# Token values of the first mix, three held rows, norms tile after tile, and background steps at the middle and end of each weight tile

## The chip, the cores and the metric

One core of a Trainium2 chip runs the whole kernel. Its engines are TensorE (PE), VectorE (DVE), ScalarE (ACT), GpSimd (POOL) and the queue of SyncE (SP), which issues DMAs. The metric is the device time of one execution in microseconds: 2220.9 us, the median of three runs of the kernel before (2220.26 to 2222.0).

## The reference, cut to what matters

Two transformer blocks run over 256 tokens of width 1024, in float32. Each is a mixing layer with a residual, followed by a product-key expert layer (PEER) with a residual.

```python
h = rmsnorm(x, norm_mix_g)                       # block 1, first mix
rq, rk, rv, rg, dq, dk, dv = split(h @ w_in)     # 4 retention heads, 4 attention heads
ret = silu(rg) * rmsnorm(retention(rq, rk, rv))
att = rmsnorm(softmax(q1 k1) @ dv - lam * softmax(q2 k2) @ dv, g) * 0.8
x = x + concat(ret, att) @ w_out
x = x + peer(rmsnorm(x, norm_ffn_g), wq, subkeys, u, v)
x = rmsnorm(x, final_norm_g)
h = rmsnorm(x, norm1_2)                          # block 2: a gated delta rule and a gated
x = x + mix(h) @ w_out_2                         # linear recurrence, 80 column tiles of w_in_2
x = x + peer(rmsnorm(x, norm2_2), w_pq, sub_keys, u_2, v_2)
return rmsnorm(x, final_norm_2)
```

`peer` picks 16 experts per token and head from 128 x 128 keys. The kernel computes it densely: `gelu(x @ u.T)` for all 16384 experts, times a matrix of gates that is zero for all experts that were not picked, times `v`.

## The kernel before

Every weight matrix is a row of tiles of 128 x 1024 floats (512 KB). `plan` lists all of them in the order of use: 28 of the first mix's `w_in`, 8 of `w_out`, 16 of `wq`, 128 of `u`, 128 of `v`, then the same for block 2. SP loads a tile into a ring of three `raw` buffers (L151). ACT copies it rounded into `hi` (L159), DVE and POOL write the rest `lo = raw - hi` (L164, DVE the first 640 columns in the mixes, POOL the others), each in a ring of three buffers. `x` is split in the same way into `xh` and `xl`, and each product is the sum of three matmuls, `hi*xh`, `hi*xl` and `lo*xh`.

`tile_ch` (L197) multiplies one tile: its 8 chunks of 128 x 128 are the stationary operands, the 256 tokens stream past, 24 matmuls of 256 columns add up in one PSUM bank, and the result has channels on the partitions. `acc_tile` (L278) does it the other way round for `v` and the output projections: the activations are stationary, 512 columns of the weight stream, tokens are on the partitions, and two token tiles (tt) with two halves of 512 columns (dh) fill four banks.

The work between the big products is written as generators in `k.bg`. `pass_round` advances each of the first four or ten by one step, and a step usually holds one stage on one engine (a group of small matmuls, then the ACT or DVE operation that reads them). In the first mix and in `Mix2` two rounds stand behind each tile. The order of instructions on an engine is then made by a scheduler from the order in the program and its own estimates of times; `issue_after(i)` makes it keep what is in the block behind instruction i on that engine.

The first mix takes its 28 tiles in the order 4 x `rg`, then `dq dk dv` of each attention head, then `rq rk rv` of each retention head. `dv` is transposed to tokens by two matmuls against the identity per head (L702). `norm_first` normalises both token tiles: a diagonal matrix of the reciprocal roots times `x` (L349), then ACT and DVE copy the 8 chunks of both token tiles out (L353, L354). Three later norms (`norm` after each mix, `norm_twice` after the first expert layer) do for each token tile: add the projection to x (L289, L291), sum of squares on ACT (L296), times the gain (L370, L385, L389), reciprocal root on POOL (L308), diagonal matrix on DVE (L300), 8 matmuls that transpose (L323), `xh` on ACT (L325), `xl` on DVE (L326). A 128 x 128 product of plain float32 counts as two matmuls in the trace. `final` does the same without the transposes, and writes out.

An output projection or `v` holds its last rows back (`LAST = 2` of 128): all rows but those are added for both token tiles, then the held rows for token tile 0, then for token tile 1, so that token tile 0's sums are complete while PE still works on tile 1. The held weights stay in the `hi` and `lo` rings.

## Time and profile before

| what | value |
|---|---|
| median of three runs | 2220.9 us |
| the profiled execution | 2218.6 us, span 2216.8 us |
| PE busy | 2167.8 us, 98% of the span, 15512 matmuls |
| DVE, ACT, POOL busy | 69%, 52%, 37% |
| mean granted TensorE clock | 0.996 of full speed |
| DMA | 167 GB/s mean |

A busy share is of the whole span and hides single stages. The idle time of PE is the difference between a stretch and PE's busy time in it. A row of the timeline gives the start, the length, the engine, the line, the operation, its output and inputs, how many are merged, and in brackets how long the engine was idle before it and what ended that. Matmuls overlap: the row's length is that of one matmul from end to end, the distance between starts is what it costs.

### The profile page before, as it was taken

How to read it: one execution, taken by the hardware profiler on the slowest of the kernel's cores; microseconds unless marked ns; L12 is line 12 of the kernel's file. 1: busy time of each engine (PE TensorE's matmuls, PEld its weight loads, DVE VectorE, ACT ScalarE, POOL GpSimd, SP SyncE). 2: the span in 40 equal slices, each digit the busy share in tenths (PEclk: the TensorE clock that was granted, in tenths of full speed). 3: DMA queues.
4: the chain of work that ended last, by engine and by line, in shares of the span. 5: the costliest groups of instructions: out<-in, count | busy, mean ns of one | idle time of the engine just before them, and what ended most of it. 6: DMA issues, size and time to landing. Idle time of an engine off the chain costs nothing. (4 is left out here: it accounts for less than half of the span.)

```text
span 2216.8 us, 41395 instructions
## 1 busy us (share of the span) xinstructions
PE 2167.8 (98%) x15512; PEld 2016.0 (91%) x15512; DVE 1533.0 (69%) x3122; ACT 1154.8 (52%) x2183; POOL 813.5 (37%) x623
## 2 busy tenths in 40 slices
PE   8999999999999999989999999999999999999998
PEld 8989999999988888879899998999999999888887
DVE  5669986898644544477687787799778885444444
ACT  5645545444455555556455655455454445555554
POOL 3454000000065666646275675620000002665664
PEclk9999999999999999999999999999999999999999
DMA  5555655555556656534444244555555555665654
GB/s 188 155 176 162 185 170 167 157 162 161 172 190 207 200 192 196 193 118 137 131 123 135 68 143 152 173 162 185 178 162 158 157 160 183 193 206 190 195 194 152
DMA packets 103880, 370.89 MB, mean 167 GB/s; under 512 B 12928, under 2 KB 14080, under 8 KB 103424
## 3 DMA queue, kind: packets, MB, share of 16 engines
q1 hardware_dynamic: 101808, 365.21, 52.1%
q10 hardware_dynamic: 1872, 3.04, 0.5%
q8 instruction: 122, 2.00, 0.4%
q14 instruction: 78, 0.64, 0.1%
HBM read 367.16 MB, written 1.05 MB: 166 GB/s over the span
## 5 line engine op out<-in xcount | busy, mean ns | idle before, releaser
L164 POOL TENSOR_TENSOR lo<-raw,hi 128x384 fp32r<-128x384 f32 (+1 forms) x428 | 689.5, 1612 | 1309.1 <-ACT hi L159 1271.4
L159 ACT ACTIVATE hi<-raw 128x1024 fp32r<-128x1024 f32 x684 | 724.0, 1060 | 680.2 <-PE mm L197 403.4
L164 DVE TENSOR_TENSOR lo<-raw,hi 128x640 fp32r<-128x640 f32 (+1 forms) x654 | 668.0, 1022 | 313.5 <-ACT hi L159 306.2
L197 PE MATMUL mm<-xh,hi 128*128 128x256 f32 x2848 | 820.9, 288 | 4.4 <-DVE sg L866 2.9
L197 PE MATMUL mm<-xh,lo 128*128 128x256 f32 x2848 | 807.5, 284 | 0.3 <-DVE lo L164 0.2
L197 PE MATMUL mm<-xl,hi 128*128 128x256 f32 x2848 | 803.9, 282 | 0.9 <-DVE xl L326 0.7
L197 PEld LDWEIGHTS mm<-xh,hi 128*128 128x128 f32 x2848 | 538.2, 189 | 5.9 <-DVE sg L866 3.3
L197 PEld LDWEIGHTS mm<-xl,hi 128*128 128x128 f32 x2848 | 538.9, 189 | 1.8 <-DVE xl L326 1.1
L197 PEld LDWEIGHTS mm<-xh,lo 128*128 128x128 f32 x2848 | 534.8, 188 | 0.7 <-DVE lo L164 0.7
L278 PE MATMUL y<-lo,ah 128*128 128x512 f32 x1024 | 398.2, 389 | 0.0
L278 PE MATMUL y<-hi,ah 128*128 128x512 f32 x1024 | 397.4, 389 | 0.0
L278 PE MATMUL y<-hi,al 128*128 128x512 f32 x1024 | 275.9, 389 | 0.0
L635 DVE TENSOR_TENSOR al<-a,ah 128x256 fp32r<-128x256 f32 x256 | 118.1, 462 | 193.2 <-PE y L278 192.9
L278 PEld LDWEIGHTS y<-hi,al 128*128 128x128 f32 x1024 | 192.2, 188 | 39.9
L278 PEld LDWEIGHTS y<-lo,ah 128*128 128x128 f32 x1024 | 192.3, 188 | 39.8
L278 PEld LDWEIGHTS y<-hi,ah 128*128 128x128 f32 x1024 | 192.2, 188 | 39.8
L634 ACT ACTIVATE ah<-a 128x256 fp32r<-128x256 f32 x256 | 106.5, 417 | 168.3 <-PE y L278 166.7
L197 PE MATMUL wm<-xh,hi 128*128 128x256 f32 x320 | 92.1, 289 | 5.4 <-ACT sq L1059 2.1
L197 PE MATMUL wm<-xh,lo 128*128 128x256 f32 x320 | 90.6, 285 | 0.6 <-DVE lo L164 0.6
L197 PE MATMUL wm<-xl,hi 128*128 128x256 f32 x320 | 90.5, 283 | 0.3 <-DVE xl L326 0.3
L535 DVE TENSOR_TENSOR ow<-ow,w 128x1024 f16<-128x1024 f16 x128 | 87.1, 683 | 0.1
L563 ACT ACTIVATE a<-mm 128x256 f32<-128x256 f32 (+33 forms) x228 | 69.0, 302 | 0.0
(513 smaller groups left out, 2271.6 us busy)
## 6 DMA issues: line engine op xcount, KB each, us to landing
raw<-in_u_dram SPq DMA_DIRECT2D x256, 512.0 KB, 3.5
raw<-in_v_dram SPq DMA_DIRECT2D x256, 512.0 KB, 4.2
raw<-in_w_in_dram SPq DMA_DIRECT2D x108, 512.0 KB, 3.5
raw<-in_wq_dram SPq DMA_DIRECT2D x32, 512.0 KB, 3.7
raw<-in_w_out_dram SPq DMA_DIRECT2D x16, 512.0 KB, 3.6
raw<-in_w_branch_a_dram SPq DMA_DIRECT2D x8, 512.0 KB, 3.5
raw<-in_w_branch_b_dram SPq DMA_DIRECT2D x8, 512.0 KB, 3.6
skT<-in_sk_dram ACTq DMA_DIRECT2D x2, 1024.0 KB, 5.1
```

Source lines behind the costliest of these rows:

```text
L159: self.nc.scalar.activation(out=h, in_=r, func=ACTF.Copy)
L164: eng.tensor_tensor(out=l[:, a:b], in0=r[:, a:b], in1=h[:, a:b].bitcast(F32), op=ALU.subtract)
L197: self.nc.tensor.matmul(out=ps, lhsT=a[:, c, :], rhs=b, start=(c == 0 and k == 0), stop=(c == NC - 1 and k == 2))
L278: i = self.nc.tensor.matmul(out=self.y[tt][dh], lhsT=p[:, ts], rhs=q[:, ds], start=(first and m == 0), stop=(last and m == 2))
L535: nc.vector.tensor_tensor(out=ow[q], in0=ow[0], in1=some(self.w[:, q]), op=ALU.mult)
L563: nc.scalar.activation(out=a[:, s, n:T], in_=ps[:, n:T], func=ACTF.Gelu)
L634: nc.scalar.activation(out=h, in_=a, func=ACTF.Copy)
L635: nc.vector.tensor_tensor(out=l, in0=a, in1=h.bitcast(F32), op=ALU.subtract)
```

## The change

Five things are changed.

1. The four tiles of `dv` come first in the first mix, in another layout (`_quads`): each holds two chunks of 128 input channels times all 512 columns of `dv`. `tile_tok` makes x the stationary operand, so the result has tokens on its partitions and 512 columns, and needs no transposes (`vt`, one ACT copy per token tile). `norm_first` is called for one token tile at a time, and its ACT and DVE copies are per chunk and token tile (128 x 128).
2. The constants `sub`, `pr` and `lam` of the attention heads are computed three rounds later, behind the last gate product on DVE and the last sigmoid on ACT.
3. `LAST = 3`, and the held rows have buffers of their own (`hold`), in the space of `a1` once that is used up. The gains are loaded there at row 72 of 128 instead of row 40.
4. `turn`: in `norm`, `norm_twice` and `final` the add, the square and the gain of a half stand together, the second half behind the first, and token tile 1 behind token tile 0's diagonal matrix (or its scaling, in `final`).
5. In the first mix's heads and in `Mix2`, one `pass_round` is called in the middle of a tile's 24 matmuls and one at its end, instead of two at the end.

```diff
     def _conv(self):
...
-        h = self.ring.tile([P, D], FR, tag="hi", name="hi", bufs=HI)
+        if n in self.place:
+            h, l = self.place.pop(n)
+        else:
+            h, l = (self.ring.tile([P, D], FR, tag=t, name=t, bufs=b) for t, b in (("hi", HI), ("lo", LO)))
...
-    def tile_ch(self, xh=None, xl=None, tag=None):
+    def tile_ch(self, xh=None, xl=None, tag=None, mid=None):
...
+            if mid is not None and c == NC // 2 - 1:
+                mid()
...
+    def tile_tok(self, tt, w, n, y):
+        h, l = w
+        ts = slice(tt * P, (tt + 1) * P)
+        todo = [(x, b, c2) for x, bs in ((self.xh, (h, l)), (self.xl, (h,))) for c2 in range(2) for b in bs]
+        for m, (x, b, c2) in enumerate(todo):
+            self.last_mm = self.nc.tensor.matmul(out=y, lhsT=x[:, 2 * n + c2, ts], rhs=b[:, c2 * 512:c2 * 512 + 512],
+                                                 start=(n == 0 and m == 0), stop=(n == 3 and m == len(todo) - 1)).ins
+
+    def first_quads(self, norms):
+
+        self.prefetch(3)
+        norms[0]()
+        ws = [self.weights() for _ in range(3)]
+        self.quads = [self.bank([P, 512])]
+        for n in range(3):
+            if n == 2:
+                norms[1]()
+            self.tile_tok(0, ws[n], n, self.quads[0][1])
+        self.quads.append(self.bank([P, 512]))
+        for n in range(3):
+            self.tile_tok(1, ws[n], n, self.quads[1][1])
+            with self.tc.issue_after(self.last_act):
+                self.prefetch(n + 1)
+        w = self.weights()
+        for tt in range(2):
+            self.tile_tok(tt, w, 3, self.quads[tt][1])
...
+    def turn(self, tt, n):
+
+        return self.tc.issue_after(self.first_half) if n else self.tc.issue_after(self.behind) if tt else nullcontext()
...
-    def norm_first(self, g, xn):
+    def norm_first(self, tt, g, xn):
...
+        for c4 in range(2):
+            tag, ps = self.bank([P, 4, P])
+            with self.tc.issue_after(self.last_mm) if tt else nullcontext():
+                for c in range(4):
+                    cc = c4 * 4 + c
+                    nc.tensor.matmul(out=ps[:, c, :], lhsT=x[:, cc * P:(cc + 1) * P], rhs=dr, start=True, stop=True)
+            for c in range(4):
+                cc = c4 * 4 + c
+                h, gc = self.xh[:, cc, ts], g[:, cc:cc + 1]
+                last = nc.scalar.activation(out=h, in_=ps[:, c, :], func=ACTF.Copy, scale=gc)
...
     def norm(self, tt, gn, xg, xn):
...
         for dh in range(2):
             hs = self.half(dh)
-            self.add_half(tt, dh, None)
-            self.square(x[:, hs], xn[:, hs], s[dh])
-        for dh in range(2):
-            hs = self.half(dh)
-            nc.vector.tensor_tensor(out=xg[:, hs], in0=x[:, hs], in1=gn[:, hs], op=ALU.mult)
+            with self.turn(tt, dh):
+                self.add_half(tt, dh, None)
+                self.square(x[:, hs], xn[:, hs], s[dh])
+                self.first_half = nc.vector.tensor_tensor(out=xg[:, hs], in0=x[:, hs], in1=gn[:, hs], op=ALU.mult).ins
...
-LAST = 2
+LAST = 3
...
-                if n == 40:
-                    gs = [k.spread(row(m), g) for m, g in enumerate(self.gs)]
-                if n == 60 and len(gs) > 1:
+                if n == P - SPLIT + 8:
+
+                    ap1.__exit__(None, None, None)
+                    end = pool("end")
+                    row = lambda name, dt=F32: end.tile([P, D], dt, name=name)
+                    gs = [k.spread(row(f"g{m}"), g) for m, g in enumerate(self.gs)]
+                    scratch = [[row(f"x{tt}{m}") for m in range(1 + len(gs))] for tt in range(2)]
+                    k.hold(P - LAST - n, [(row(f"wh{m}", FR), row(f"wl{m}", FR)) for m in range(LAST)])
+                if n == P - 40 and len(gs) > 1:
...
-                k.prefetch()
-
-            held = [(k.weights(), a) for a in last]
+                k.prefetch(2 + (n > P - LAST - 5))
+
+            held = [(k.weights(), a) for a in parts]
...
-        k.norm_first(k.g, [pool.tile([P, D], F32, name="xn", tag="xn", bufs=2) for tt in range(2)])
-        k.prefetch_behind()
+        k.first_quads([lambda tt=tt: k.norm_first(tt, k.g, pool.tile([P, D], F32, name="xn", tag="xn", bufs=2)) for tt in range(2)])
+        vt = pool.tile([P, 2, 4, P], F32, name="vt")
+        for tt, (tag, ps) in enumerate(k.quads):
+            nc.scalar.activation(out=vt[:, tt].rearrange("p h n -> p (h n)"), in_=ps, func=ACTF.Copy)
+            k.done(tag)
+        k.prefetch()
...
-        nc.vector.tensor_scalar(out=sub, in0=sub, scalar1=1.0 - (0.8 - 0.6), scalar2=None, op0=ALU.mult)
...
-        def lam_last():
+        def lambdas():
             yield
             yield
+            yield
+            pr = pool.tile([P, 2, 64], F32, name="pr")
+            d2 = dl.rearrange("p (a two) b -> p a two b", two=2)
+            with k.tc.issue_after(gate):
+                nc.vector.tensor_tensor(out=pr, in0=d2[:, :, 0, :], in1=d2[:, :, 1, :], op=ALU.mult)
+                nc.vector.tensor_reduce(out=lam[:, 0:2], in_=pr, axis=AX.X, op=ALU.add)
+                nc.vector.tensor_scalar(out=sub, in0=sub, scalar1=1.0 - (0.8 - 0.6), scalar2=None, op0=ALU.mult)
+            with k.tc.issue_after(sig):
...
-                for n in "qkv":
-                    ps = k.tile_ch()
+                names = "qk" if kind == "d" else "qkv"
+                for n in names:
+                    ps = k.tile_ch(mid=lambda: pass_round(k, 4))
                     got.append(halves(ps) if kind + n == "dq" else taken(ps, kind + n))
-                    if n == "v":
+                    if n == names[-1]:
                         k.spawn(work(h, *got))
-                    pass_round(k, 4)
                     pass_round(k, 4)
...
+
+        mid = self.mid = lambda: pass_round(k, 10)
+
+        def after():
+            pass_round(k, 10)
...
-                ps, done = k.tile_wide()
+                ps, done = k.tile_wide(mid)
...
-            after(2)
+            after()
...
+def _quads(w):
+
+    return np.ascontiguousarray(w.reshape(4, 2, P, 512).transpose(0, 2, 1, 3)).reshape(4, P, D)
```

How the rows of an engine move is seen best at three places. First, PE at the start of the program: `by_93` to `by_96`, `by_112`, `by_125`, `by_158` and `bg_171` are banks of transposes, `by_138` is the bank of token tile 0's `dv`. Before:

```order
L349 MATMUL by_95<-xn,x 128x128 x2
L349 MATMUL by_96<-xn,x 128x128 x2
L197 MATMUL mm<-xh,hi 128x256
L197 MATMUL mm<-xl,hi 128x256
L197 MATMUL mm<-xh,lo 128x256
```

and now, from the first matmul of the program:

```order
L395 MATMUL by_112<-xn,x 128x128 x4
L395 MATMUL by_125<-xn,x 128x128 x4
L218 MATMUL by_138<-hi,xh 128x512
L218 MATMUL by_138<-lo,xh 128x512
L218 MATMUL by_138<-hi,xh 128x512
L218 MATMUL by_138<-lo,xh 128x512
L218 MATMUL by_138<-hi,xl 128x512 x2
L218 MATMUL by_138<-hi,xh 128x512
L218 MATMUL by_138<-lo,xh 128x512
L218 MATMUL by_138<-hi,xh 128x512
L218 MATMUL by_138<-lo,xh 128x512
L218 MATMUL by_138<-hi,xl 128x512 x2
```

Products stood behind the transposes of both token tiles; now 12 products of token tile 0 stand before the transposes of token tile 1.

Second, DVE at the norm after the second mix, from the halves of token tile 0 on. Before:

```order
L370 TENSOR_TENSOR xg<-x,gn 128x512 x2
L289 TENSOR_TENSOR x<-y,x 128x512
L371 TENSOR_SCALAR nrm<-nrm 128x1
L289 TENSOR_TENSOR x<-y,x 128x512
L370 TENSOR_TENSOR xg<-x,gn 128x512
L300 TENSOR_SCALAR xn<-k_ident,nrm 128x128
L370 TENSOR_TENSOR xg<-x,gn 128x512
L371 TENSOR_SCALAR nrm<-nrm 128x1
L300 TENSOR_SCALAR xn<-k_ident,nrm 128x128
L326 TENSOR_TENSOR xl<-bg_16445,xh 128x4x128
```

and now, from the second half of token tile 0 on:

```order
L328 TENSOR_TENSOR x<-y,x 128x512
L416 TENSOR_TENSOR xg<-x,gn 128x512
L417 TENSOR_SCALAR nrm<-nrm 128x1
L343 TENSOR_SCALAR xn<-k_ident,nrm 128x128
L328 TENSOR_TENSOR x<-y,x 128x512
L416 TENSOR_TENSOR xg<-x,gn 128x512
L328 TENSOR_TENSOR x<-y,x 128x512
L369 TENSOR_TENSOR xl<-bg_16398,xh 128x4x128
L416 TENSOR_TENSOR xg<-x,gn 128x512
L417 TENSOR_SCALAR nrm<-nrm 128x1
L369 TENSOR_TENSOR xl<-bg_16405,xh 128x4x128
L343 TENSOR_SCALAR xn<-k_ident,nrm 128x128
```

Both adds of token tile 1 stood ahead of token tile 0's diagonal matrix (`xn`); now they stand behind it, with two `xl` of token tile 0 between them and token tile 1's diagonal matrix.

Third, PE at the end of the program. `y_22760` and `y_22761` are token tile 0's two halves before, `y_22713` and `y_22714` now. Before:

```order
L278 MATMUL y_22760<-hi_25656,ah_25579 128x512
L278 MATMUL y_22761<-hi_25656,ah_25579 128x512
L278 MATMUL y_22760<-lo_25658,ah_25579 128x512
L278 MATMUL y_22760<-hi_25656,al_25580 128x512
L278 MATMUL y_22761<-lo_25658,ah_25579 128x512
L278 MATMUL y_22761<-hi_25656,al_25580 128x512
L278 MATMUL y_22762<-hi_25639,ah_25575 128x512
```

and now:

```order
L317 MATMUL y_22713<-wh2_24387,al_25593 128x512
L317 MATMUL y_22714<-wh0_24383,al_25585 128x512
L317 MATMUL y_22714<-wh1_24385,ah_25588 128x512
L317 MATMUL y_22714<-wl1_24386,ah_25588 128x512
L317 MATMUL y_22714<-wh1_24385,al_25589 128x512
L317 MATMUL y_22714<-wh2_24387,ah_25592 128x512
L317 MATMUL y_22714<-wl2_24388,ah_25592 128x512
L317 MATMUL y_22714<-wh2_24387,al_25593 128x512
L317 MATMUL y_22715<-wh0_24383,ah_25584 128x512
```

Token tile 0's halves were complete with 14 and 12 matmuls left to do; now they are with 25 and 18 left.

## Rows read from the trace of the kernel before

**Rows 1.** Stretches (us): length, busy (count) of PE, PEld, DVE, ACT, POOL; granted clock; DMA.

```profile
13.10:33.20 20.10, 16.97 (x124) 16.30 (x123) 11.05 (x22) 12.12 (x19) 9.08 (x6) 0.92 0.59 177
33.20:140.80 107.60, 107.27 (x789) 101.31 (x788) 66.83 (x110) 60.28 (x146) 46.56 (x38) 1.00 0.53 162
...
147.50:952.30 804.80, 804.46 (x5573) 740.90 (x5573) 550.63 (x1136) 411.81 (x721) 250.71 (x145) 1.00 0.57 181
952.30:964.00 11.70, 5.77 (x35) 5.60 (x34) 7.61 (x20) 5.87 (x15) 4.66 (x7) 0.71 0.03 14
964.00:1360.00 396.00, 375.64 (x3091) 362.55 (x3092) 304.84 (x625) 221.42 (x514) 226.92 (x258) 1.00 0.40 124
```

**Rows 2.** The timeline at the start, first norm to first product.

```profile
6.74 6.62 PE L349 MATMUL by<-xn,x 128*128 128x128 f32 x32 [6.74 <-DVE xn L300]
...
7.35 1.06 ACT L159 ACTIVATE hi<-raw 128x1024 fp32r<-128x1024 f32 x1 [0.57 <-DMA raw<-in_w_in_dram]
...
12.27 2.70 ACT L353 ACTIVATE xh<-by,i_norm_mix_g 128x256 fp32r<-128x256 f32 x7 [0.38 <-PE by L349]
...
13.12 0.37 PE L197 MATMUL mm<-xh,hi 128*128 128x256 f32 x1
```

**Rows 3.** POOL's share of a conversion: count | busy, mean ns | idle before it.

```profile
L164 POOL TENSOR_TENSOR lo<-raw,hi 128x384 fp32r<-128x384 f32 (+1 forms) x428 | 689.5, 1612 | 1309.1 <-ACT hi L159 1271.4
```

**Rows 4.** The timeline around the fifth tile of the first mix, on DVE.

```profile
25.38 0.15 DVE L742 TENSOR_SCALAR sub<-sub 128x1 f32<-128x1 f32 x1 [2.28 <-DMA sub<-in_diff_subln_g_dram]
```

**Rows 5.** The same stretch on PE.

```profile
28.68 0.38 PE L197 MATMUL mm<-xh,hi 128*128 128x256 f32 x1 [2.38 <-DVE sg L866]
```

**Rows 6.** The stretch behind it, columns as in Rows 1.

```profile
29.60:33.20 3.60, 3.60 (x20) 3.60 (x19) 0.83 (x1) 1.06 (x1) 1.65 (x1) 0.53 0.46 166
```

**Rows 7.** The chain of waits: start, length, what (long runs of products).

```profile
1821.13 40.37 PE mm L197 x336
1861.50 345.01 PE y L278 x1522
```

**Rows 8.** PE at the norm after the first expert layer.

```profile
957.89 3.76 PE L323 MATMUL bg<-a 128*128 128x128 f32 x16 [5.59 <-issue]
...
963.95 0.39 PE L197 MATMUL wm<-xl,hi 128*128 128x256 f32 x1 [0.34 <-DVE xl L326]
```

**Rows 9.** DVE at the norm after the second mix.

```profile
1395.86 1.29 DVE L289 TENSOR_TENSOR x<-y,x 128x512 f32<-128x512 f32 x2 [0.59 <-PE y L278]
...
1402.41 0.69 DVE L326 TENSOR_TENSOR xl<-bg,xh 128x512 fp32r<-128x512 f32 x1 [0.26 <-ACT xh L325]
```

**Rows 10.** PE at the norm after the second mix.

```profile
1400.61 2.02 PE L323 MATMUL bg<-xn,xg 128*128 128x128 f32 x16 [1.77 <-DVE xn L300]
1402.47 1.95 PE L323 MATMUL by<-xn,xg 128*128 128x128 f32 x16
...
1404.94 0.39 PE L197 MATMUL mm<-xl,hi 128*128 128x256 f32 x1 [0.34 <-DVE xl L326]
```

**Rows 11.** PE at the norm after the first mix.

```profile
143.22 2.02 PE L323 MATMUL bg<-xn,xg 128*128 128x128 f32 x16 [2.45 <-DVE xn L300]
...
147.55 0.39 PE L197 MATMUL mm<-xl,hi 128*128 128x256 f32 x1 [0.34 <-DVE xl L326]
```

**Rows 12.** DVE at the end of the program: the adds of token tile 0.

```profile
2206.53 1.29 DVE L291 SCALAR_TENSOR_TENSOR x<-y,x 128x512 f32<-128x512 f32 x2 [3.02 <-PE y L278]
```

**Rows 13.** ACT at the end of the program: the last square, the last scaling.

```profile
2211.03 0.61 ACT L296 ACTIVATE a<-x 128x512 f32<-128x512 f32 x1
...
2212.78 0.72 ACT L304 ACTIVATE a<-a,nrm 128x512 f32<-128x512 f32 x1 [1.04 <-POOL nrm L308]
```

**Rows 14.** What PE waited for from 964 to 1360 us: us in total, times, longest.

```profile
PE wm L197 <- ACT sq L1059: 2.1, 2, 1.2
PE by L1054 <- DVE qc L1049: 1.9, 2, 1.4
...
PE mm L197 <- DVE lo L164: 0.2, 1, 0.2
```

More of the change, by code (lines that the diff above doesn't have):

```diff
@@ L175, in prefetch, with hold @@
             self._dma()
+    def hold(self, n, homes):
+        for m, home in enumerate(homes):
+            assert self.n_use + n + m >= self.n_cv
+            self.place[self.n_use + n + m] = home
     def weights(self):
@@ L333, in prefetch_behind @@
             self.prefetch(ahead)
-    def norm_first(self, g, xn):
+    def norm_first(self, tt, g, xn):
         nc = self.nc
-        banks = [self.bank([P, 2, 2, P]) for c2 in range(4)]
-        for tt in range(2):
-            x, s = self.x[:, tt, :], self.columns()
-            self.square(x[:, 512:D], xn[tt][:, 512:D], s[0])
-            nc.vector.scalar_tensor_tensor(out=xn[tt][:, 0:512], in0=x[:, 0:512], scalar=1.0 / D, in1=x[:, 0:512],
-                                           op0=ALU.mult, op1=ALU.mult, accum_out=s[1])
-            nc.vector.tensor_scalar(out=s[4], in0=s[0], scalar1=s[1], scalar2=EPS, op0=ALU.add, op1=ALU.add)
-            self.rsqrt(s[6], s[4])
-            dr = xn[tt][:, 0:P]
-            self.diagonal(dr, s[6])
-            for c in range(NC):
-                nc.tensor.matmul(out=banks[c // 2][1][:, c % 2, tt, :], lhsT=x[:, c * P:(c + 1) * P], rhs=dr, start=True, stop=True)
-        for c in range(NC):
-            tag, ps = banks[c // 2]
-            v, h = ps[:, c % 2].rearrange("p a b -> p (a b)"), self.xh[:, c, :]
-            last = nc.scalar.activation(out=h, in_=v, func=ACTF.Copy, scale=g[:, c:c + 1])
-            nc.vector.scalar_tensor_tensor(out=self.xl[:, c, :], in0=v, scalar=g[:, c:c + 1], in1=h.bitcast(F32),
-                                           op0=ALU.mult, op1=ALU.subtract)
-            if c % 2:
-                self.done(tag)
@@ new lines, in norm_first @@
+        x, s = self.x[:, tt, :], self.columns()
+        self.square(x[:, 512:D], xn[:, 512:D], s[0])
+        nc.vector.scalar_tensor_tensor(out=xn[:, 0:512], in0=x[:, 0:512], scalar=1.0 / D, in1=x[:, 0:512],
+                                       op0=ALU.mult, op1=ALU.mult, accum_out=s[1])
+        nc.vector.tensor_scalar(out=s[4], in0=s[0], scalar1=s[1], scalar2=EPS, op0=ALU.add, op1=ALU.add)
+        self.rsqrt(s[6], s[4])
+        dr = xn[:, 0:P]
+        self.diagonal(dr, s[6])
+        ts = slice(tt * P, (tt + 1) * P)
@@ new lines, in norm_first @@
+        for c4 in range(2):
[8 more added lines that the diff above has]
+                last = nc.scalar.activation(out=h, in_=ps[:, c, :], func=ACTF.Copy, scale=gc)
+                with self.tc.issue_after(self.behind) if tt else nullcontext():
+                    i = nc.vector.scalar_tensor_tensor(out=self.xl[:, cc, ts], in0=ps[:, c, :], scalar=gc, in1=h.bitcast(F32),
+                                                       op0=ALU.mult, op1=ALU.subtract).ins
+            self.done(tag)
@@ L358, in norm_first @@
         self.last_act = last.ins
+        self.behind = i
     def norm(self, tt, gn, xg, xn):
@@ L412, in final @@
             hs = self.half(dh)
-            self.add_half(tt, dh, scale)
-            self.square(x[:, hs], xn[:, hs], s[dh])
-        for dh in range(2):
-            hs = self.half(dh)
-            nc.vector.tensor_tensor(out=xg[:, hs], in0=x[:, hs], in1=gb[:, hs], op=ALU.mult)
+            with self.turn(tt, dh):
+                self.add_half(tt, dh, scale)
+                self.square(x[:, hs], xn[:, hs], s[dh])
+                self.first_half = nc.vector.tensor_tensor(out=xg[:, hs], in0=x[:, hs], in1=gb[:, hs], op=ALU.mult).ins
         nc.vector.tensor_scalar(out=s[4], in0=s[0], scalar1=s[1], scalar2=EPS, op0=ALU.add, op1=ALU.add)
@@ L680, in run @@
             for tt in range(2):
-                after(tt, 1.0 / GS, *gs, *(row(len(gs) + 3 * tt + m) for m in range(3)))
+                after(tt, 1.0 / GS, *gs, *scratch[tt])
             if k.n_use < len(k.plan):
@@ L909 @@
 MIX1_OUT = [4, 5, 6, 7, 0, 1, 2, 3]
[L910 removed]
+MIX1_TILES = [12, 13, 14, 15] + [b + h for h in range(4) for b in (16, 20)] + [b + h for h in range(4) for b in (0, 4, 8)]
 H = 8
@@ L1441, in run @@
         self.bi, self.sgb = self.t([P, 2, H, P], "bi"), self.t([P, H, T], "sgb")
-        def after(n=1):
-            for _ in range(n):
-                pass_round(k, 10)
+        mid = self.mid = lambda: pass_round(k, 10)
+        def after():
+            pass_round(k, 10)
             k.prefetch()
@@ L1473, in run @@
         for h in range(H):
-            ps, done = k.tile_wide()
+            ps, done = k.tile_wide(mid)
             silu(ps, self.qb[:, h, :])
             done()
-            after(2)
+            after()
         with k.tc.issue_after(self.last_sigmoid):
```

84 lines of the change are left out of this document (38 added, 46 removed).

## The prediction

> **What bounds the kernel now.** I read the stretches by stage first, then the chain of waits, then the timeline where a stretch had idle time. The chain's two long runs are PE alone: 336 products of 256 columns in 40.37 us, 0.120 each, and 1522 of 512 columns in 345.01 us, 0.227 each [rows 7]. Between the norms of the expert layers PE idles 0.3 of 804.8 us, and in the heads of the first mix 0.3 of 107.6 [rows 1]: there only fewer matmuls can save time. The idle time lies in four kinds of places: before the first product at 13.12 us [rows 2]; 3.1 us between 13.1 and 33.2, with a granted clock of 0.92 [rows 1]; at each norm (5.59, 1.77 and 2.45 us before the first transposes [rows 8, 10, 11]); and 20.4 us in the second mix, which the waits list splits into 28 waits in 22 kinds, 20.1 us in all, 0.72 each, none over 1.5 [rows 1, 14]. The change touches all four.
>
> **Start and first mix.** Before, PE makes all 32 transposes (6.62 us, 0.207 each), then ACT copies 256 columns at a time (7 in 2.70, 0.39 each), and products begin at 13.12 [rows 2]. Now token tile 0's 16 transposes end at 6.74 + 3.3 = 10.05. ACT has the first `hi` until 8.41, then two more at 1.06 and eight copies of 128 columns, not shown, between half of 0.39 and 0.39; I take 0.3, nearer the whole since each has a start-up: 8.41 + 2.1 + 2.4 = 12.9. The 12 products that stand first (12 x 0.227 = 2.7) end with the last copy and its `xl`, about 13.5. The second token tile's transposes (2.0 by [rows 10]) end at 15.5, and 36 products more (8.2) at 23.7. The three held weight tiles fill the rings, so the fourth conversion waits until the first has been used twice; PE waits some 0.6 for it: 24.3.
>
> Then come four gate tiles and the first `dq`, five tiles: 5 x 24 x 0.120 = 14.4, which gives 38.7. Before, those five are done at 33.2, 5.7 us later than 13.12 + 14.4. Of these 5.7, 2.38 are a wait for a gate product on DVE [rows 5] that stood in DVE's queue behind `sub`, which waited for its DMA [rows 4], and 3.6 x 0.47 = 1.7 are the half clock behind it [rows 6]. Both go: `sub` and `pr` now stand behind the last gate product, when their loads have long landed. But before still has four `dv` tiles to do (96 x 0.120 = 11.5) and eight transposes (8 x 0.126 = 1.0): the gain is 33.2 + 12.5 - 38.7 = 7.0. An attention head now gives the chain of its softmax two tiles of cover instead of three; I take 1.0 of new waits there, so **-6.0**. Bounds: with no wait at all 24.3 becomes 10.05 + 48 x 0.227 + 2.0 = 22.9, and no wait in the heads: -8.4. If each of the next four conversions comes whole behind its ring slot (1.06 [rows 2] + 1.61 on POOL [rows 3], four times 2.7), PE waits 10.7 instead of 0.6: +4 with the heads' 1.0.
>
> **Norms in order.** The new wait is on DVE: token tile 1's first add stands behind token tile 0's diagonal matrix, so all of tile 1 is queued there while ACT's square, DVE's small sum and POOL's root run, and PE's second transposes wait for it. From the last square's start to the operation that uses the root is 2212.78 - 2211.03 = 1.75 us [rows 13]; a DVE operation on 512 columns costs 0.60 in a row [rows 9, 12].
> Norm after the second mix, T = 1400.61 - 1.77 = 1398.84, the end of PE's sums. The first add starts at T-2.98 [rows 9]; add, gain, add, of which the second add ends at T-1.18, its square starts at once, the diagonal matrix follows 1.75 later and takes 0.3: T+0.9, first transposes at T+0.95 against T+1.77. DVE then does add, gain, add (1.8), an `xl` of tile 0 (0.7), the last gain (0.6): T+4.0; sum, root and matrix 1.25 more: T+5.25, second transposes there against T+3.63. From there the steady products start 2.47 later [rows 10]: T+7.7 against T+6.1: **+1.6**. Norm after the first mix the same, against 147.55 - 140.77 = 6.8: **+0.9**. Bounds for the two together: 0 if the scheduler's other order of `xl` makes up for it, +5 if ACT's squares queue behind the copies.
> Norm after the first expert layer: three held rows. Token tile 0's halves are complete with 25 and 18 matmuls left, T-5.5 and T-3.9 (with 0.17 of the last one's tail), instead of 14 and 12. Six DVE operations 3.6, the last squares, two small ones: the matrix is done at T, just when PE gets free (T = 957.89 - 5.59 = 952.30), and PE does not pause. Tile 1: six DVE operations 3.6, two `xl` 1.4, then 1.5: T+6.6, and 2.47 later T+9.05, against 963.95 - 952.30 = 11.65: **-2.6**. Bounds: -4.5 (no `xl` between) and 0.
> End of the program: the first scaling at T-1.5, tile 1's adds done at T+0.85, square to scaling 1.75, scaling 0.72: T+3.3, against 2213.50 - 2209.68 = 3.8 (T is 14 x 0.227 after 2206.51 [rows 7, 12]): **-0.5**, bounds -1 and +0.5.
>
> The trace has one more thing to say here: after the gap of 5.59 us the clock of the stretch is 0.71 [rows 1, 8], after 2.38 us 0.53 [rows 6], but after 2.45 and 1.77 us the transposes run at 0.116 apiece [rows 10, 11]. The new order leaves PE a gap of 2.4 us between the transposes of the two token tiles in two norms, and of 4.7 in the third. The Trainium skill ("TensorE: Matmul & The Clock Gate", "HAM oscillation — how this bites in real kernels") says that gaps in which TensorE idles take its full clock from the work behind them. By that rule this part of the change costs more than the sum says; it is the second rival, and the rows are split on it.
>
> **Held rows and loads.** The held rows' own buffers free the rings, but ACT's order puts the first held conversion before the conversion of the row ahead of it, and the last held row's load waits for a `raw` buffer: 0.3 each time, **+0.6**, bounds 0 and +4 (a whole load late, twice). The gains' loads go down SP's queue 32 rows later, in a stretch where PE idles 0.3 of 805 us, and are used 50 rows after: nothing.
>
> **Rounds at the middle and the end.** Instructions and rounds are the same in number. Two steps that stood back to back now have 12 products (1.44 us) between them, twice the mean wait of 0.72, so some of the 28 waits should go; but the scheduler moved steps apart before already, and the order of the second mix has small matmuls at 117 places between products instead of 108. I take **-1.0**; from both sides it is -20.1 (all waits go) and +20.1 (as many again). In the heads of the first mix PE has 0.3 us to give.
>
> **Sum.** -6.0 + 1.6 + 0.9 - 2.6 - 0.5 + 0.6 - 1.0 = -7.0. The profiled execution took 2218.6, and 2211.6 would follow; it lies 2.3 under the median of 2220.9, from which I predict **2214**.
>
> **Rivals.**
> First, the weights of the first mix come late: the rings are full of the three tiles used twice, the wait of 0.6 grows to 5, the start gains 1 to 2, and the time is about 2218.5. For it: conversions of the fourth to the seventh tile must fit behind 16 small copies on ACT. Against: ACT is 60% busy there [rows 1].
> Second, the clock: transposes behind the new gaps at 0.207 instead of 0.116, 16 x 0.09 = 1.5 in each of three norms: -7.0 + 4.4 gives 2218.3. For it [rows 6, 8], against it [rows 10, 11].
> Third, the second mix gains: half of its waits go, 10 instead of 1: 2205. For it: most of its waits are for DVE or ACT operations of the step just before [rows 14].
> Fourth, **slower**: the second mix waits more. A step in the middle of a tile stands among products that add up in one bank, and PE takes its queue in order; DVE is 77% busy in this stretch [rows 1], so a step's DVE part can come later than 1.44 us. With 0.72 per wait, ten more waits eat the 7.0; 22 more, about the twofold, give 2214 + 1 + 15 = 2230. Against it: the same work, with more distance between the steps.
> That the change does not do what it says I can exclude from the order: `dv` has no transposes, three rows are held.
>
> **Chances.** Forecast 0.52, first rival 0.14, second 0.12, third 0.14, fourth 0.08. The measurement tells 0.2% (4.4 us) from no change, so faster means below 2216.5: nine tenths of the forecast, the third rival and a third of the first two, 0.69; slower 0.06, the rest is the same. The forecast's own range is 2209 to 2218; eight in ten with the rivals' ends: 2205 to 2220.
>
> **What would show it.** Right: the first 512-column product near 10 us and the first gate tile near 24; no wait for `sg` above 1 us before 45 us and no half clock there; steady products 9 us after PE's last sum at the norm after the first expert layer, and 7.7 after the other two; the last scaling 3.3 us after PE's last sum. Wrong: a first gate tile after 28; a clock below 1 behind the norms; idle time in the second mix below 12 or above 28 us, which would move the total by more than all norms together.

## The result, and the profile after

The changed kernel takes 2235.0 us, the median of four runs, against 2221.5 for the kernel before on the same chip: a ratio of 1.0069, 95% interval [1.0057, 1.0082]. It is slower by 13.6 us between the medians, by 15 us by the ratio, where 2214 was forecast. The profiled execution took 2235.64 us (span 2233.9, mean granted clock 0.992); the one before had 2218.6, 2216.8 and 0.996.

The stretches of the kernel after, cut at the same places as the stages of the prediction (columns as in [rows 1]). Most cuts lie at PE's last sum of a projection or of `v` (its last matmul there) and at the start of the steady products behind the norm:

```profile
0.00:24.90 24.90, 18.14 (x82) 15.41 (x83) 12.53 (x31) 14.43 (x28) 10.72 (x12) 1.00 0.57 191
...
111.40:140.00 28.60, 26.57 (x116) 20.95 (x115) 15.22 (x22) 10.52 (x19) 12.99 (x10) 0.94 0.51 166
140.00:147.00 7.00, 4.37 (x36) 4.01 (x35) 4.56 (x10) 3.73 (x9) 0.56 (x1) 1.00 0.00 0
147.00:953.80 806.80, 804.74 (x5573) 740.51 (x5572) 555.92 (x1139) 412.01 (x722) 249.56 (x145) 1.00 0.57 181
953.80:964.90 11.10, 5.69 (x35) 5.41 (x35) 6.62 (x15) 4.30 (x11) 4.34 (x6) 0.85 0.00 0
964.90:1410.50 445.60, 422.43 (x3328) 406.39 (x3327) 330.34 (x664) 242.00 (x538) 250.84 (x272) 0.97 0.40 126
1410.50:1418.90 8.40, 4.62 (x36) 4.16 (x36) 5.46 (x12) 3.83 (x9) 1.11 (x2) 1.00 0.06 21
1418.90:2227.20 808.30, 804.96 (x5573) 740.61 (x5572) 548.34 (x1137) 410.84 (x719) 247.85 (x144) 1.00 0.56 177
2227.20:2233.90 6.70, 0.22 (x1) 0.00 (x0) 2.34 (x5) 1.79 (x5) 0.55 (x1) 0.81 0.40 150
```

The second mix with its output projection, before, between the same places:

```profile
964.20:1398.70 434.50, 414.14 (x3327) 396.64 (x3326) 333.75 (x662) 239.08 (x537) 248.30 (x272) 1.00 0.42 129
```

Set beside the same stages of before (first column), and of three of the experiments told below, in us (one profiled execution each, cut to some 0.2 us):

| stage | before | after | e7, first mix alone | e3, old norms | g1, best |
|---|---|---|---|---|---|
| to PE's last sum of the first mix | 140.6 | 140.0 | 138.2 | 137.6 | 136.2 |
| norm | 7.2 | 7.0 | 6.5 | 6.5 | 6.5 |
| first expert layer | 804.4 | 806.8 | 804.8 | 807.4 | 806.0 |
| norm behind it | 12.0 | 11.1 | 11.8 | 7.9 | 7.2 |
| second mix | 434.5 | 445.6 | 434.8 | 443.6 | 435.2 |
| norm | 6.5 | 8.4 | 6.5 | 6.5 | 6.5 |
| second expert layer | 804.4 | 808.3 | 804.6 | 807.7 | 807.0 |
| end | 7.3 | 6.7 | 7.3 | 6.6 | 6.6 |
| span | 2216.8 | 2233.9 | 2214.4 | 2223.7 | 2211.2 |

Of the 17.1 us, 11.1 are lost in the second mix and 6.3 in the two expert layers; the first mix gives 0.6 instead of 6. The three norms and the end together change by 0.2.

**Second mix.** Idle time grows by only 2.8 us (20.4 to 23.2), busy time by 8.3, with the same matmuls: they ran slower. Windows of the kernel after:

```profile
1009.40:1012.80 3.40, 3.15 (x14) 3.15 (x15) 3.40 (x8) 0.77 (x3) 0.52 (x1) 0.51 0.88 264
1081.00:1087.50 6.50, 5.30 (x29) 5.30 (x30) 3.83 (x9) 1.50 (x3) 0.00 (x0) 0.51 0.36 122
1108.20:1115.00 6.80, 6.80 (x34) 6.68 (x34) 0.69 (x1) 0.30 (x1) 0.00 (x0) 0.52 0.01 2
1231.00:1238.00 7.00, 6.63 (x32) 6.42 (x31) 4.97 (x15) 3.63 (x13) 4.07 (x8) 0.52 0.22 76
1347.00:1350.50 3.50, 3.30 (x16) 3.30 (x17) 1.55 (x3) 3.50 (x12) 2.32 (x2) 0.55 0.32 98
```

The granted clock is at half, 1.2 instead of 2.4 GHz, in these five stretches, 27 us in all ("half clock" below); the kernel before had one, of 3.4 us near 1222. What PE waited for from 966 to 1365 us (us in total, times, longest):

```profile
PE by L1183 <- DVE X L1341: 4.2, 2, 2.2
PE mm L206 <- DVE lo L167: 2.3, 1, 2.3
PE mm L206 <- ACT mx L1563: 2.2, 1, 2.2
PE wm L206 <- ACT kt L1118: 1.6, 1, 1.6
```

The waits are fewer and longer than in [rows 14], where none was above 1.5. Three of the five stretches begin at such a wait: 1009 (kt), 1081 (X), 1347 (mx). The one at 1108 has 0.5 us of idle time in the two us ahead of it, the one at 1231 nearly none. Two more waits as long, for `lo` (2.3, until 1170.7) and the second one for `X` (2.2, until 1202), have full clock behind them: a wait of 2 us went with half clock in some places only.

**Held rows.** ACT at the end of the second expert layer, after:

```profile
2205.85 1.06 ACT L163 ACTIVATE hi<-raw 128x1024 fp32r<-128x1024 f32 x1 [0.54 <-PE y L317]
...
2210.18 1.06 ACT L163 ACTIVATE wh<-raw 128x1024 fp32r<-128x1024 f32 x1 [2.14 <-DMA raw<-in_v_dram]
2211.14 1.04 ACT L163 ACTIVATE hi<-raw 128x1024 fp32r<-128x1024 f32 x1
...
2216.68 1.06 ACT L163 ACTIVATE wh<-raw 128x1024 fp32r<-128x1024 f32 x1 [2.69 <-DMA raw<-in_v_dram]
2217.64 0.40 ACT L678 ACTIVATE ah<-a 128x256 fp32r<-128x256 f32 x1
```

and PE:

```profile
2218.09 0.50 PE L317 MATMUL y<-wh,ah 128*128 128x512 f32 x1 [1.45 <-ACT ah L678]
...
2219.80 0.51 PE L317 MATMUL y<-wh,al 128*128 128x512 f32 x1 [0.52 <-DVE al L679]
```

ACT takes its queue in order. A held conversion (`wh`) waits there for its load, and behind it stands first a conversion whose load is there (`hi`, 2211.14), at the end the small copy `ah` that PE waits for.

**First mix.** The same thing in the output projection. ACT, then PE:

```profile
131.95 1.06 ACT L163 ACTIVATE hi<-raw 128x1024 fp32r<-128x1024 f32 x1 [2.02 <-DMA raw<-in_wq_dram]
132.91 0.40 ACT L822 ACTIVATE ch<-fy 128x256 fp32r<-128x256 f32 x1
```

```profile
133.37 0.50 PE L317 MATMUL y<-hi,ch 128*128 128x512 f32 x1 [1.52 <-ACT ch L822]
...
135.07 0.76 PE L317 MATMUL y<-hi,cl 128*128 128x512 f32 x2 [0.52 <-DVE cl L823]
```

Behind the two waits the clock is at half for 3.4 us.

### The profile page after: what moved, and what is told of

It reads as the page before. It is cut to its first block, busy times and chain, and to the rows that moved or that the text cites. A ratio compares the mean times of both kernels' runs of the same rounds, so it can differ in the third digit from the quotient of the medians.

```text
span 2233.9 us, 41262 instructions
## 1 busy us (share of the span) xinstructions
PE 2176.4 (97%) x15456; PEld 2020.9 (90%) x15456; DVE 1532.4 (69%) x3130; ACT 1156.5 (52%) x2185; POOL 820.8 (37%) x623
## 5 line engine op out<-in xcount | busy, mean ns | idle before, releaser
L167 DVE TENSOR_TENSOR lo<-raw,hi 128x640 fp32r<-128x640 f32 (+1 forms) x648 | 656.4, 1013 | 319.5 <-ACT hi L163 314.9
L206 PE MATMUL mm<-xh,lo 128*128 128x256 f32 x2816 | 798.7, 284 | 2.4 <-DVE lo L167 2.3
L206 PE MATMUL mm<-xl,hi 128*128 128x256 f32 x2816 | 794.8, 282 | 0.7 <-DVE xl L369 0.7
L206 PEld LDWEIGHTS mm<-xh,hi 128*128 128x128 f32 x2816 | 532.2, 189 | 6.5 <-ACT a L607 2.2
L206 PEld LDWEIGHTS mm<-xh,lo 128*128 128x128 f32 x2816 | 529.2, 188 | 3.0 <-DVE lo L167 2.8
L317 PE MATMUL y<-lo,ah 128*128 128x512 f32 x1000 | 387.9, 389 | 0.0
L317 PE MATMUL y<-hi,ah 128*128 128x512 f32 x1000 | 387.7, 389 | 0.0
L317 PE MATMUL y<-hi,al 128*128 128x512 f32 x1000 | 267.6, 389 | 0.0
```

The lines of the kernel that those rows point to most:

```text
L167: eng.tensor_tensor(out=l[:, a:b], in0=r[:, a:b], in1=h[:, a:b].bitcast(F32), op=ALU.subtract)
L206: self.nc.tensor.matmul(out=ps, lhsT=a[:, c, :], rhs=b, start=(c == 0 and k == 0), stop=(c == NC - 1 and k == 2))
L317: i = self.nc.tensor.matmul(out=self.y[tt][dh], lhsT=p[:, ts], rhs=q[:, ds], start=(first and m == 0), stop=(last and m == 2))
```

## Experiments

Ratios are to the kernel before, run beside each on the same chip, with 95% intervals; 0.001 is 2.2 us. A difference of two ratios is uncertain by some 3 to 4 us. Stages and stretches at half clock are those of the one profiled execution of each kernel. Each kernel is the changed one with the edits named; e7, g2 and so on are the labels of the runs.

### The first mix alone (e7)

Rounds at the end in both mixes, two held rows, norms as before: only parts 1 and 2 of the change are left.

> The kernel before with only the first mix by tokens and the later constants: rounds at the end in both mixes, two held rows, norms as before. Theory (what the start gains is lost again in the output projection, where the last retention head's chain ends late): first gate tile near 25 us, the last weight tile of the heads done 4 to 5 us earlier than before, but waits of 1.5 to 4 us in the output projection, and the time 0 to 4 us under the kernel before: about 2219.5 (2217 to 2222). Rival (the rounds in the middle caused those waits): no wait above 0.5 us there, 5 to 6 us gained, 2215 to 2217. Second rival (the sum of the other parts is not additive): above 2223.

1.0005 [0.9996, 1.0014], 2220.3 us. PE's last sum comes at 138.2, 2.4 us earlier than before, not 6. The heads end 5 us earlier (their last product starts at 111.2 instead of 116.3), and in the output projection PE waits 1.5 and 0.5 us. The rounds in the heads' middle did not cause those waits.

### The rounds of the second mix (e1, g2, g4)

e1 undoes the rounds alone; g2 does them alone, on e7; g4 moves the middle round nearer to the tile's start (and has the heads' rounds at the end).

```diff
-        mid = self.mid = lambda: pass_round(k, 10)
+        mid = self.mid = None
         def after():
             pass_round(k, 10)
+            pass_round(k, 10)
```

> The changed kernel with one thing undone: in the second mix both rounds stand at the end of each weight tile again. Theory (the rounds in the middle are the main loss): between the norms around it the second mix took 445.5 us in the changed kernel and 434.9 before, 10.6 more, of which 7.8 are PE busy longer at half clock and 2.8 more idle time. Undone, the mix takes 434 to 437, the half clock stays in one stretch near 1220 us, and the kernel takes about 2224.5 (2222 to 2227). Rival (the mix suffers from something else that changed, such as the later start or the order that the scheduler picks around it): less than 3 us come back, 2232 or more.

1.0045 [1.0032, 1.0058], 2229.0 us. The mix is back at 435.4:

```profile
967.10:1402.50 435.40, 414.62 (x3329) 397.37 (x3327) 333.69 (x664) 239.92 (x538) 250.89 (x272) 0.99 0.40 129
```

Some of the 10 us came out again elsewhere: this execution has 809 us in the first expert layer, and half clock from 145.8 and from 1408.7 us, behind the norms in order after both mixes, where the changed kernel's profile has full clock behind the same waits (first norm 8.6 us, 7.0 after). PE in e1, then in the changed kernel:

```profile
1408.10 3.23 PE L366 MATMUL by<-xn,xg 128*128 128x128 f32 x16 [2.29 <-DVE xn L343]
```

```profile
1416.09 2.02 PE L366 MATMUL by<-xn,xg 128*128 128x128 f32 x16 [2.30 <-DVE xn L343]
```

> The first mix by tokens (e7) and, of the other parts, only the rounds in the middle of the second mix's tiles. Theory (they cost about 10 us in the profiled mix, 7 to 8 of it as a lower clock): second mix 443 to 447 us against 434.8, 20 to 32 us of it at half clock against 3.4, mean clock about 0.992, the time 2228 (2226 to 2231) against 2220.3. Rival (they cost only together with the norms in order, since the run that undid them alone gave back 6 us and the one that undid the norms 9.5): 2223 or less.

1.0019 [1.0010, 1.0028], 2226.1 us:

```profile
961.30:1402.80 441.50, 419.48 (x3327) 403.29 (x3326) 329.52 (x662) 241.15 (x537) 250.26 (x272) 0.98 0.40 127
```

6.7 us longer than in e7, of which 5.4 are busy time; 20.5 us at half clock against 3.4. So the rounds cost by themselves, 3 us by the ratios and 6.5 by the spans of the two profiles, less than in the changed kernel. One stretch at half clock goes with them: it begins between 1096 and 1110 us, among matmuls of 64 columns and behind waits of at most 0.6 us, in all seven profiles with middle rounds in every tile of the mix (the changed kernel, e2, e3, g2, g4, h1, h2) and in none of the ten others.

```diff
-            if mid is not None and c == NC // 2 - 1:
+            if mid is not None and c == 0:
```

> The changed kernel, with the heads' rounds at the end, and the second mix's round in the middle moved to behind the first 3 of a tile's 24 matmuls, so that it is nearly back to back with the round at the end of the tile before. Theory (what costs is the distance: with 12 products between two rounds a step's DVE or ACT part has 12 products of cover instead of 21 to 24 before the next step's matmuls need it): near the kernel with both rounds at the end (2229.0), 2227 to 2231. Rival (what costs is that a step stands inside a tile's sums, where a wait holds up the tile): as the changed kernel, 2233 to 2237.

1.0068 [1.0054, 1.0081], 2237.5 us; second mix 446.4, 32 us at half clock, idle 21.3, in a profiled execution that was the slowest of five (2243.1). The theory of the distance falls: with the round behind the first 3 matmuls instead of 12 nothing came back. That a step stands inside a tile's sums is left; why it costs is not settled by this.

### Conversions ahead of the middle round (h1, h2)

```diff
-        mid = self.mid = lambda: pass_round(k, 10)
+        def mid():
+            k.prefetch()
+            pass_round(k, 10)
```

> g2 (rounds in the middle alone, 2226.1 us), with the next weight tile's conversion issued in the middle of a tile, ahead of the round there, instead of behind the round at the end. Theory (waits for late conversions let the clock fall): the waits for lo (2.3 and 1.3 us) and hi (1.1) go, half clock in the second mix falls from 20.5 us to 7 or less, and the time to about 2219 (2217 to 2222). Rival (the clock falls at the chains of small matmuls, near 1103 and 1226 us, whatever the conversions do): those two stretches stay, 13 us or more at half clock, 2223 or more.

1.0032 [1.0021, 1.0044], 2226.6 us. The edit moved conversions, but not those that PE waits for; the list of waits keeps them:

```profile
PE mm L206 <- DVE lo L167: 2.3, 1, 2.3
PE mm L206 <- ACT mx L1568: 2.2, 1, 2.2
PE wm L206 <- ACT kt L1119: 1.6, 1, 1.6
```

Half clock stays, 27 us. Since the waits didn't go, this doesn't tell the two theories apart.

> The same edit on the kernel with three held rows loaded early (f3), middle rounds in all tiles. Theory: second mix 433 to 438 us, 2213 (2211 to 2217), as good as the middle rounds in nine tiles alone (2213.0). Rival: half clock stays near 1100 and 1225 us, 2218 or more.

1.0021 [1.0012, 1.0031], 2224.5 us, 24 us at half clock, the three waits kept: the same holds.

### The norms (e3, g3)

```diff
-            with self.turn(tt, dh):
-                self.add_half(tt, dh, None)
-                self.square(x[:, hs], xn[:, hs], s[dh])
-                self.first_half = nc.vector.tensor_tensor(out=xg[:, hs], in0=x[:, hs], in1=gn[:, hs], op=ALU.mult).ins
+            self.add_half(tt, dh, None)
+            self.square(x[:, hs], xn[:, hs], s[dh])
+        for dh in range(2):
+            hs = self.half(dh)
+            nc.vector.tensor_tensor(out=xg[:, hs], in0=x[:, hs], in1=gn[:, hs], op=ALU.mult)
```

(and so in the other two norms)

> The changed kernel with the norms undone: adds and squares of both halves first, then the gains, and no order between the token tiles. Theory (order between token tiles makes the second tile late): the norm after the second mix goes from 8.3 us back to about 6.1, the one after the first mix from 6.5 to 6.8 or less, and the norm after the first expert layer, where PE waits 4.4 us for the second token tile, from 11.2 to 9 to 12: in all 1 to 4 us back, about 2232.5 (2231 to 2234). Rival (the order saves more than it costs): 2236 or more.

1.0029 [1.0017, 1.0040], 2225.5 us: 9 us come back, more than expected. The norm after the first expert layer, after and in e3 (PE):

```profile
954.92 2.02 PE L366 MATMUL bg<-x,x 128*128 128x128 f32 x16 [0.98 <-DVE x L343]
961.38 3.50 PE L366 MATMUL by<-x,x 128*128 128x128 f32 x16 [4.44 <-DVE x L343]
...
964.89 0.37 PE L206 MATMUL wm<-xl,hi 128*128 128x256 f32 x1
```

```profile
953.78 2.02 PE L366 MATMUL bg<-x,x 128*128 128x128 f32 x16 [2.09 <-DVE x L343]
956.61 2.02 PE L366 MATMUL by<-x,x 128*128 128x128 f32 x16 [0.81 <-DVE x L343]
...
959.15 0.39 PE L206 MATMUL wm<-xl,hi 128*128 128x256 f32 x1 [0.34 <-DVE xl L369]
```

Without the order the first token tile's transposes start 1.1 us later after PE's last sum (2.3 instead of 1.2) and the second's 2.5 earlier, and 16 transposes don't fall into half clock (2.02 instead of 3.50): 7.9 instead of 11.1. The norm after the second mix gives 1.9. The two mixes give the other 4 us; half clock is 20.5 us there in e3, 31 after. So the order of the norms, not the rounds, is the part whose undoing gave back most.

> The first mix by tokens (e7) and, of the other parts, only the norms in order, with two held rows. Theory (the second token tile comes late): 8.4 us instead of 6.5 in the norms after both mixes, 12.9 instead of 11.75 after the first expert layer, about 1.5 more at the end: 5 to 6 us slower than e7, 2226 (2224 to 2228). Rival (the order costs only what the two norms show, the rest of the 9.5 us was chance of the clock): 2222 to 2224.

1.0037 [1.0024, 1.0050], 2228.5 us, 7 us above e7: 8.4 instead of 6.5 in two norms, 13.3 instead of 11.8 behind the first expert layer, 8.9 instead of 7.3 at the end; then 3.4 in the second mix, where 6.8 us at half clock near 981 are new.

### The held rows (e2, f1, f2)

```diff
-LAST = 3
+LAST = 2
```

(and the held rows in the rings, the gains at row 40, as before)

> The changed kernel with the held rows undone: two held rows in the rings, the gains loaded at row 40. Theory (third held row's load and conversion late): the expert layers were 2.1 and 3.9 us longer than before, PE waits 1.3 to 1.5 and 0.5 us at the first held row behind a conversion that waits for its load. Undone, each has 804.8 us again: 6.0 back, less 0.5 to 1 in the norm after the first expert layer, which then has less cover: about 2229.5 (2228 to 2231). Rival (the stretch is longer for another reason, the ring of three weight tiles or the gains' loads at row 72): not told from it by the time alone, but then PE's wait at the first held row stays. Second rival (held rows pay for themselves through the norm): 2235 or more.

1.0069 [1.0055, 1.0084], 2234.2 us: nothing back. Both layers are back at 804.6, as the first theory has it, but with the norms in order the norm behind the first layer is 12.9 us instead of 11.1 and the end 8.9 instead of 6.7; the rest is clock (32 us at half clock in the second mix). Three held rows pay in the norm and at the end about what they cost at their loads.

> The first mix by tokens and three held rows, with the norms and the rounds of the kernel before. Theory (the third held row saves in the norm what it loses at its load): by the run with the norms undone, the expert layers are 2.6 to 3.0 us longer than before, the norm after the first one is 7.9 us instead of 11.75, the end 0.7 shorter: together within 1 us of the first mix alone (2220.3 in its run), 2221 (2218 to 2224), and PE waits for the held row's ah behind a held conversion. Rival (the longer layers came from the rounds or the order in the norms, not from the held rows): both layers back at 804.8, 2215 to 2216.

1.0012 [1.0002, 1.0022], 2222.1 us. So it is without the order: norm 6.9 instead of 11.8, layers 5.0 and 2.0 longer than before, in sum nothing clear of the spread against e7 (1.0005).

```diff
+                    for m in range(1, LAST):
+                        r = row(f"raw{m}")
+                        nc.sync.dma_start(out=r, in_=k.plan[k.n_use + P - LAST - n + m])
+                        k.raw[k.n_use + P - LAST - n + m] = r
```

> The same, and the second and third held rows are loaded at row 88 into buffers of their own instead of behind row 124's through the ring. Theory (their loads come late since they wait for a ring buffer, and ACT's held conversion with all that stands behind it waits for the load): no wait for a load on ACT at the end of either layer, no wait of PE for ah or al there, both layers within 0.5 us of 804.8, the norm still near 7.9: 5 us under the run beside it, about 2215.5 (2213 to 2218). Rival (ACT's order, not the load, makes ah late): the wait at the first held row stays above 1 us and less than 2 us come back.

0.9991 [0.9982, 1.0000], 2217.6 us, 0.0021 or 4.7 us below f1. ACT at the end of the second expert layer, then PE:

```profile
2197.50 1.06 ACT L166 ACTIVATE wh<-raw 128x1024 fp32r<-128x1024 f32 x1 [2.25 <-DMA raw<-in_v_dram]
...
2200.28 0.42 ACT L684 ACTIVATE ah<-a 128x256 fp32r<-128x256 f32 x1 [0.46 <-PE y L320]
```

```profile
2202.80 1.07 PE L320 MATMUL y<-hi,al 128*128 128x512 f32 x4
2203.70 0.40 PE L320 MATMUL y<-wh,ah 128*128 128x512 f32 x1
```

The wait on PE is gone, so its cause was the load. The first held row's conversion still waits for its load on ACT (2.25), but early enough. 3.0 and 1.8 us of the two layers' excess stay: PE waits 0.9 and 0.4 us some 640 us into a layer, near the place where the two held rows are now loaded among the others, and 1.1 and 0.6 some 110 us into it.

### The copy before the conversion (f3)

```diff
-    k.prefetch(1)
+    with k.tc.issue_after(k.last_ch):
+        k.prefetch(1)
```

> The same, and in the first mix's output projection the conversion of the next weight tile stands behind the last head's copy on ACT. Theory (that copy, ready at 131.4, stood behind a conversion that waited for its load until 131.7, and PE waited 1.5 and 0.5 us for it): both waits go, the first mix is 2 us shorter (136 instead of 138.2 at PE's last sum), about 2213.5 (2211 to 2216). Rival (the chain of the last head is what is late, the copy only its last link): the wait moves to the head's DVE operations and stays above 1 us, nothing gained.

0.9990 [0.9981, 0.9999], 2217.6 us. ACT now does the copy first:

```profile
130.92 0.42 ACT L834 ACTIVATE ch<-fy 128x256 fp32r<-128x256 f32 x1 [1.23 <-DVE fy L833]
131.82 1.06 ACT L166 ACTIVATE hi<-raw 128x1024 fp32r<-128x1024 f32 x1 [0.49 <-DMA raw<-in_wq_dram]
```

PE waits for nothing in the output projection, and its last sum comes at 135.7 (137.0 in f2, 138.2 in e7). The cause of the waits is shown; the time is the same as f2's: in the profiles the norm behind it takes 0.8 longer, and the rest lies within the spread.

### Middle rounds in some tiles (f4, g1, h3)

```diff
+        first = k.n_use
+        early = lambda: k.n_use - first <= N
-        mid = self.mid = lambda: pass_round(k, 10)
+        mid = self.mid = lambda: early() and pass_round(k, 10)
         def after():
             pass_round(k, 10)
+            early() or pass_round(k, 10)
```

f4 has N = 32, g1 has N = 9, both on f3.

> The same, with a round in the middle and one at the end in the first 32 weight tiles of the second mix alone. By the tile times of the changed kernel against the one before, those 32 tiles went 5.1 us faster there, and the next 64 lost 15.6, with half clock at 1081, 1108, 1231 and 1347 us. Theory (the loss lies in the later tiles, where the steps are chains of small matmuls): the second mix takes 430 to 433 us instead of 435, about 2211 (2208 to 2214). Rival (the early tiles only put off steps that the later ones then do): 435 or more and no gain.

1.0009 [0.9999, 1.0018], 2221.1 us, half clock at 1001 and 1072 us. The second mix takes 440.8 us, as the rival has it: no gain.

> f3 with rounds in the middle and at the end in the first 9 weight tiles of the second mix alone. By the tile times the changed kernel gained 5.0 us against the kernel before up to the tenth tile and lost 4.0 in the next two, behind a wait of 2.55 us. Theory (the stretch after the norm gains, since there the waits of 2.5 us near 981 split): no half clock near 978, second mix 434 to 437 instead of 440.8, 2213.5 (2211 to 2216). Rival (the steps put off by the middle rounds come back as a wait right behind, as in f4): 2217 or more.

0.9963 [0.9950, 0.9976], 2213.0 us: 8 us faster than the kernel before, the best of all. f3 has 6.8 us of half clock near 976 and as much near 1215; g1 has none at either place, and 3.4 us each near 1000 and 1045:

```profile
956.00:1391.10 435.10, 414.35 (x3327) 397.87 (x3326) 334.01 (x664) 239.00 (x537) 250.54 (x272) 0.99 0.41 129
```

> g1 (middle rounds in the first nine tiles, 2213.0 us) with the conversion in the middle of every tile of the second mix. Theory: the waits for conversions that are left there (some 1 us) go, 2212 (2210 to 2214). Rival (an earlier conversion stands ahead of a step's operation on ACT and DVE and delays that instead): 2215 or more.

0.9969 [0.9957, 0.9980], 2213.8 us: the same as g1.

## Why the prediction was wrong, point by point

The forecast was 7 us faster; it came out some 15 us slower. Each part by its stages in the profile, alone on top of e7, and undone in the changed kernel (us, the last two from ratios, each uncertain by 2 to 4):

| part | forecast | its stages, after against before | alone | given back when undone |
|---|---|---|---|---|
| start and first mix | -6.0 | -0.6 | +1 (e7) | not run |
| rounds | -1.0 | +11.1 | +3 (g2) | 5 (e1) |
| norms in order, with the third held row's cover | -0.6 | +0.2 | +7 (g3, two held rows) | 9 (e3) |
| held rows and loads | +0.6 | +6.3 | +2 (f1, with the norm's gain) | 0 (e2) |

- **Rounds, -1.0: the step that failed by most.** The second mix took 11.1 us longer in the profiles; by the ratios of g2 over e7 and of the changed kernel over e1 the rounds account for 3 to 5 of them, and no run says what the others belong to. "Some of the 28 waits should go": they became fewer, but longer, and the idle time grew by 2.8 us. The bound of +20.1 held it, the value taken did not. The fourth rival named the place and priced it by waits at 0.72; its 22 new waits were not what came. What both left out was the clock: a price for half clock stood in [rows 6], and was not set against waits of 2 us that might form. The idle time, 23.2 us, even lay within the 12 to 28 that the prediction named as its sign; the loss was in busy time. Why the clock fell where it did stays open.
- **Start and first mix, -6.0: measured -0.6, the second step that failed.** The start was right: first product of 512 columns at 10.19, first gate tile from 23.3 and in one piece from 24.9, no half clock by 45 us; one wait for `sg`, of 1.3 us, is above the 1 us that the prediction allowed. The heads end 5 us earlier. Then nothing was asked of the output projection: the last head's copy stands on ACT behind a conversion that waits for its load (f3), 2.0 us of waits and 3.4 us at half clock behind them. The bound of +4 covered the first weights only.
- **Held rows and loads, +0.6: measured +2.4 and +3.9, the third, mis-sized.** The mechanism was right (held conversion ahead on ACT, last load waits for a buffer; f2 shows it), the size was not: not 0.3 each, but 2 us, and `ah` queued behind it. The bound was +4 for both. 1.2 us of the second layer's excess is another wait, for a gelu behind a late conversion and two table loads on ACT, 112 us into it (before, the same table loads stood there without a wait of PE).
- **Norms in order: +1.6, +0.9, -2.6, -0.5; measured +1.9, -0.2, -0.9, -0.6.** In sum 0.8 off. After the first expert layer PE paused 0.98 us before the first transposes, where no pause was taken, and half clock made the second tile's transposes 1.5 us longer. The -0.2 is luck: with PE late in the projection, the first token tile was ready (1.9 more than e7 in g3). The sum came near because the gain of the third held row was put down to the order: the old norms with three held rows take 7.9 instead of 11.1 (e3), so against them the order loses at that norm.
- **Second rival, the clock behind norm gaps (0.12).** Of the 16 transposes behind 2.29 and 2.30 us of waiting none was slowed in the profile of the changed kernel, those behind 4.44 were; in e1 the same code had half clock behind both waits of 2.29. So its mechanism exists, and the rows were rightly split on it. The Trainium skill ("TensorE: Matmul & The Clock Gate", "HAM oscillation — how this bites in real kernels") says that gaps take the clock from the work behind them; the trace agrees at 1009, 1081 and 1347 us and at 4.44, not behind 2.29 and 2.30 nor behind the waits that end at 1170.7 and 1202, and at 1231 the clock fell where PE was idle for less than 0.4.
- **First and third rival.** Weights were not late at the start. Half of the second mix's waits did not go.
- The range, 2205 to 2220, left out 2235. Its upper end took in none of the parts' upper bounds (+4, +5, +4, +20.1), of which the third was passed and the last reached by half.

## What to carry to other kernels

Ask of each wait that a change may lengthen not only what it costs, but whether the clock may fall behind it: here 2.8 us of idle time came with 8.3 us of slower matmuls. Judge a part by runs with it alone and with it undone: the stages of single profiles put 11 us on the rounds and nothing on the norms, the ratios 3 to 5 and 7 to 9. An engine that takes its queue in order should not have a conversion that waits for a load ahead of a small copy that the bottleneck waits for; a load into a buffer of its own, or an order that puts the copy first, ended the wait in both places. A part of a change that loses in sum can win at one place: the middle rounds in nine of 88 tiles were worth 6 us (g1 against f3), in all of them they lost 3 (g2 against e7).

## What the runs showed of the hardware

Stretches at half clock lasted 3.4, 6.8 or 10.2 us in every kernel, but for those that the program's end cut off. Executions of one kernel differ by the clock: of e7's eleven, the one at 2216.3 us had a mean granted clock of 0.998, the one at 2225.3 had 0.994. The same wait went with half clock in one kernel's profile and with full clock in another's: the 2.3 us between the two token tiles' transposes after the mixes had half clock behind it in e1 and g4, not in the changed kernel, e2 and g3; the 2.1 to 2.3 us for `lo` near 1170 had it in e2, g4, h1 and h2, not in the changed kernel, e3 and g2. So such a wait alone does not decide it. Half clock begins between 1214 and 1240 us in 14 of the 17 profiles, before included, in a stretch of small matmuls of 64 columns, with no idle time ahead of it in the kernel before and hardly any after; what lowers the clock there stays open.
